# An encoder block on one core: VectorE work reordered at three places of the attention and gate stages

## The chip, the core and the metric

The kernel runs on one core of a Trainium2 chip. A core has five engines, each with its own instruction queue: TensorE (PE; its weight loads are shown apart as PEld), VectorE (DVE), ScalarE (ACT), GpSimd (POOL) and SyncE (SP), which here issues nearly all DMAs. They wait for one another on semaphores. The metric is the device time of one execution in microseconds (us); the median of three runs is given.

## What is computed

One block of a bidirectional encoder for 1024 tokens of 1024 features, in 32-bit floats. Cut to what matters:

```
h    = layer_norm(x)
proj = h @ w_in + b_in                  # split into qa ka va | qb kb vb | ga gb
y_na  = neighbourhood_attention(qa, ka, va, rpb) @ w_branch_na     # 8 heads of 64
y_swa = windowed_gqa_with_sink(qb, kb, vb, sink) @ w_branch_swa    # 8 query heads, 2 key heads
mixed = sigmoid(ga) * y_na + sigmoid(gb) * y_swa
h = layer_norm(ALPHA * h + mixed @ w_out + b_out)
h = layer_norm(ALPHA * h + square(relu(h @ w_ff1 + b_ff1)) @ w_ff2 + b_ff2)
```

## The kernel before

Matmul operands are split into two parts: a high part, the value rounded to the type that PE multiplies fast, and a low part, the rest. A product is three matmuls: high by high, high by low, low by high. So every operand costs ACT a rounding copy (high) and DVE a subtraction (low). Partial sums lie in PSUM, in banks of 128 x 512: four tags (`mm`, `s`, `t`, `o`) of two banks each.

The order of the work on every engine is written out by hand (`manual_schedule`): what the code calls first stands first in its engine's queue.

**Attention.** 16 heads of 4 steps each, 64 steps; the first 8 heads are the windowed ones, the last 8 the neighbourhood's. Step `s` (function `steps`) issues, in this order:

- `part_a2(s + 1)`: DVE turns the sums of exponentials into reciprocals (L592, L593) and scales two tiles of weights with them (L596).
- `part_a(s + 2)`: PE computes scores in two `s` banks (L559, L560); DVE adds the mask or bias, writes the tile out and takes the row maxima (L562), then their negative (L566, L568). These read the banks and so free them.
- a first share of the pumps (below), then a flush of early deferred work,
- `part_b(s)`: PE turns the weights (transposes, L618) into two `t` banks; ACT copies them rounded (`pth`, L621); between, `part_e` lets ACT take the exponentials of step `s + 2` (L580, L583); then DVE takes the low parts (`ptl`, L624), which free the `t` banks; then a flush,
- a second share of the pumps,
- `part_c(s - 1)`: PE multiplies weights and values (L654) into an `o` bank, which takes two steps. After the second, ACT copies one half of the bank's partitions into `oT` (L660), and DVE adds the other half to it (L663, the output addition); then a flush and the last share of the pumps.

A pump is one matmul (L283) of the projections, which fill PE between the attention's own matmuls. A step has 12 pumps in the first 8 heads and 18 in the last 8. Work on a projection's result is deferred: `defer(n, f, ...)` puts `f` on a list to be called at the first flush after `n` more pumps. A flush goes through the list; the flush ahead of `part_b` takes only entries marked early.

For the neighbourhood's q and k (`proj_na_qk`), each half projection ends in `evac` (three copies on ACT) and, four pumps later, `evac2` (three operations on DVE: the low part of q, L358, that of k, L360, and a copy of the latter, L362). The first two read the `mm` bank of the projection and so free it. Both are marked early.

**Gates.** After the attention the remaining columns of the gates' projection are multiplied by a seven-product scheme: operands A11 to A22 and the sums S1 to S4 of activations against sums of weights. `g_sums` forms a weight sum on DVE (L856), `g_hi` rounds it on ACT (L872), `g_lo` takes its low part on DVE (L876), `g_mm` multiplies (L886), and `g_after` brings a result out: a copy on ACT (L946) or an addition on DVE (L926). The sums of activations use helper `f_add` (L926 too). Product 7 uses S3, which is formed into the place of an operand used up, `hT`, in two halves of 1024 columns: ACT rounds both (L1045), then DVE takes both low parts. Products 7 and 4 of one weight block use one bank, with the addition of product 7's result in between.

After the gates come the branch projections, the output projection with its layer norm, and the two feed-forward matrices in the same seven-product scheme. The change touches nothing there.

Of the kernel before, what the change touches and what calls it, by code (L numbers as in the profile page):

```python
# [13 lines left out]
ALU = mybir.AluOpType  # L14
# [33 lines left out]
D_NA = 4  # L48
# [35 lines left out]
def encoder_block(ctx, tc, x, w_in, w_br, w_out, w_ff1, w_ff2, par, rows, rpbp,  # L84
# [4 lines left out]
    def b32(ap):  # L89
        return ap.bitcast(F32)  # L90
# [12 lines left out]
    def psum(tag):  # L103
        return pp.tile([P, 512], F32, tag=tag, name=f"ps_{tag}", bufs=PSB[tag])
# [153 lines left out]
    def h_perm(part, k, half):  # L258
        return hT[:, part, k, half * 512:(half + 1) * 512]
# [17 lines left out]
    def gemm3_steps(ps, w, act):  # L277

        hi, lo = w[:2]
        for k in range(NK):  # L280
            for i, (a, b) in enumerate(((hi, 0), (hi, 1), (lo, 0))):
                yield
                PE.matmul(ps, a[:, k, :], act(b, k), start=(k == 0 and i == 0), stop=(k == NK - 1 and i == 2))  # L283
# [6 lines left out]
    def defer(*fns, pe=False, early=False):  # L290

        later.append([fns[0], fns[1:], pe, early])
# [48 lines left out]
    def proj_na_qk(h, w, store):  # L341
        q = ap.tile([P, S], F32R, tag="q", name="q", bufs=3)
        kh = ap.tile([P, S], F32R, tag="kh", name="kh")
        kl = ap.tile([P, S], F32R, tag="kl", name="kl")
        store.append((q, kh, kl))
        bq, bk = prm[0:64, C_QK + h:C_QK + h + 1], prm[64:P, C_QK + h:C_QK + h + 1]
        for half in range(2):
            cs = slice(half * 512, (half + 1) * 512)
            ps = psum("mm")
            yield from gemm3_steps(ps, w, lambda part, k: h_perm(part, k, half))  # L350

            def evac(cs=cs, ps=ps):
                ACT.activation(q[0:64, cs], ps[0:64, :], AF.Identity, bias=bq, scale=1.0)
                ACT.activation(kh[64:P, cs], ps[64:P, :], AF.Identity, bias=bk, scale=1.0)
                ACT.activation(kh[0:64, cs], ps[64:P, :], AF.Identity, bias=bk, scale=1.0)

            def evac2(cs=cs, ps=ps):
                DVE.scalar_tensor_tensor(out=q[64:P, cs], in0=ps[0:64, :], scalar=bq, in1=b32(q[0:64, cs]),  # L358
                                         op0=ALU.add, op1=ALU.subtract)
                DVE.scalar_tensor_tensor(out=kl[64:P, cs], in0=ps[64:P, :], scalar=bk, in1=b32(kh[64:P, cs]),  # L360
                                         op0=ALU.add, op1=ALU.subtract)
                DVE.tensor_copy(kl[0:64, cs], b32(kl[64:P, cs]))  # L362
            defer(0, evac, D_NA, evac2, early=True)


    mk = ap.tile([P, 640], F32, tag="mk", name="mk", bufs=1)
# [20 lines left out]

    n_rope = [0]
    in_steps, rope_ops = [], []

    def rope_step(p):

        if rope_ops:
            j = cp.tile([P, 1], F32, tag="junk", name="junk", bufs=2)
            POOL.tensor_copy(j, p[:, 0:1])
            rope_ops.pop(0)()
            if len(rope_ops) % 5 == 1:
                rope_ops.pop(0)()
                if rope_ops:
                    defer(8, rope_ops.pop(0))  # L400
# [184 lines left out]
    def part_a2(s):  # L585
        if s >= 64:
            return
        hd, t = heads[s // 4], s % 4
        pns, st = hd.pairs[t]
        sink_h = hd.get()[4]  # L590
        if sink_h is not None:
            DVE.tensor_tensor(out=st[:, 4:6], in0=st[:, 4:6], in1=st[:, 6:8], op=ALU.add)  # L592
        DVE.reciprocal(out=st[:, 6:8], in_=st[:, 4:6])  # L593
        for i in range(2):
            p, n, c0 = pns[i]
            DVE.tensor_scalar(out=p[:, :n], in0=p[:, :n], scalar1=st[:, 6 + i:7 + i], scalar2=None, op0=ALU.mult)  # L596
        rope_step(p)
# [29 lines left out]
    def part_c(s):  # L627

        hd, t = heads[s // 4], s % 4
        order, pth, ptl = hd.pairs[t]  # L630
        _, vv, vi, _, _, o_chunk, o_row = hd.get()
        if t % 2 == 0:
            hd.po = psum("o")
        po = hd.po

        runs = []
        for u, (c, i) in enumerate(order):
            if runs and runs[-1][0] == c:
                runs[-1][2] += 1
            else:  # L640
                runs.append([c, u, 1, i])
        runs.sort(key=lambda r: -r[2])
        runs.append(runs.pop(1))
        cols_ = (t % 2) * 256
        nmm = 0
        for c, u, w, i in runs:
            cc = slice(cols_ + i * P, cols_ + (i + w) * P)
            vs = vv[:, c, vi, :, :].rearrange("p a f -> p (a f)")
            main = (po[:, cc], vs, pth[:, u:u + w, :].rearrange("p u f -> p (u f)"))
            corr = (po[0:64, cc], vs[:, 0:64], ptl[:, u:u + w, :].rearrange("p u f -> p (u f)"))  # L650
            nmm += 1
            lastrun = nmm == len(runs)
            for m in ((corr, main) if lastrun else (main, corr)):
                PE.matmul(*m, start=(nmm == 1 and m is main), stop=(lastrun and m is main))  # L654
        if t % 2 == 1:

            oo = oT[o_row:o_row + 64, o_chunk, (t // 2) * 512:(t // 2 + 1) * 512]

            def evac():
                ACT.copy(oo, po[64:P, :])  # L660

            def evac2():
                DVE.tensor_tensor(out=oo, in0=po[0:64, :], in1=oo, op=ALU.add)  # L663
            if s == 63:
                last_evac.extend((evac, evac2))
            else:
                evac()
                defer(0, evac2)

    def fills():  # L670
        def na_v_of(hp):
# [28 lines left out]
    with tc.manual_schedule(engines=MANUAL):  # L700
# [22 lines left out]
        def pump(n):  # L723
            for _ in range(n):
                if next(fill, "end") == "end":
                    for e in later:
                        e[0] = 0
                    flush()
                    return
                for e in later:  # L730
                    e[0] -= 1
# [52 lines left out]
        def steps(s, n, before_b=None, before_c=None):  # L784

            part = [int(n * SPLIT[0]), int(n * SPLIT[1])]
            part.append(n - sum(part))
            if 0 <= s + 1 < 64:
                part_a2(s + 1)
            if s + 2 < 64:  # L790
                part_a(s + 2)
            pump(part[0])
            if before_b:
                before_b()
            flush(False, True)
            if 0 <= s < 64:
                part_b(s, lambda: part_e(s + 2))
            elif s < 0:
                part_e(s + 2)
            flush(False)  # L800
            pump(part[1])
            if before_c:
                before_c()
            if s >= 1:
                part_c(s - 1)
            flush()
            pump(part[2])
# [45 lines left out]
        def g_sums(p, i):  # L853

            def sub(out, a, b):
                DVE.tensor_tensor(out=out, in0=a, in1=b, op=ALU.subtract)  # L856
            if i == 6:
                gT2[p] = gp.tile([P, 4, P], F32, tag="ts", name="gT2")
                sub(gB(p, 1, 1), gB(p, 1, 2), gB(p, 1, 1))
                sub(gT2[p], gB(p, 2, 2), gB(p, 1, 1))  # L860
            elif i == 7:
                sub(gB(p, 1, 2), gB(p, 2, 2), gB(p, 1, 2))
            elif i == 4:
                sub(gB(p, 2, 1), gB(p, 2, 1), gT2[p])
# [4 lines left out]
        def g_hi(p, i, src=None):  # L869
            gtags.append(gtags.pop(0))  # L870
            t = gw[p, i] = wp.tile([P, 2, 4, P], F32R, tag=gtags[-1], name="gw", bufs=1)
            ACT.copy(t[:, 0], g_src(p, i) if src is None else src)  # L872

        def g_lo(p, i, src=None):
            t = gw[p, i]
            DVE.tensor_tensor(out=t[:, 1], in0=g_src(p, i) if src is None else src, in1=b32(t[:, 0]), op=ALU.subtract)  # L876
# [13 lines left out]
        gop = dict(A11=hT[:, :, K1, T1], A12=hT[:, :, K2, T1], A22=hT[:, :, K2, T2], S3=hT[:, :, K1, T2])  # L890
# [34 lines left out]
        def f_add(out, a, b, op=ALU.add):  # L925
            DVE.tensor_tensor(out=out, in0=a, in1=b, op=op)  # L926
# [10 lines left out]
        g2 = gt[:, 0].rearrange("p (a x) -> p a x", a=4)  # L937
# [103 lines left out]
        g_lo(3, 3)  # L1041
        g_do(2, 5)
        g_do(3, 5)
        for ks in (slice(0, 2), slice(2, 4)):
            ACT.copy(gop["S3"][:, 0, ks], g2[:, ks])  # L1045
        g_sums(2, 7)
        g_sums(3, 7)
        g_hi(2, 7)
        for ks in (slice(0, 2), slice(2, 4)):
            f_add(gop["S3"][:, 1, ks], g2[:, ks], b32(gop["S3"][:, 0, ks]), ALU.subtract)  # L1050
        g_lo(2, 7)
        g_hi(3, 7)
        g_lo(3, 7)
        g_sums(2, 4)
# [1006 lines left out]
```

## Time and profile before

| | |
|---|---|
| median of three runs | 1334.39 us (1333.94 to 1335.63) |
| profiled execution | 1334.06 us |
| its span, first to last instruction | 1332.3 us |
| granted TensorE clock, mean | 0.998 |
| PE busy | 1309.4 us, 6296 matmuls |
| DVE busy | 985.0 us |
| ACT busy | 710.1 us |
| POOL busy | 282.4 us |
| attention, first score product to last | about 91 to 436 us of the span |

The profile is one execution. Times in it are us from the span's start; a row of a timeline gives start, duration, engine, line, operation, what is written and read, the shape, how many instructions were merged, and in brackets the idle time of the engine before it with what ended it. The ends of matmuls are modelled: one of 128 x 512 is shown with some 0.39 us, while the next starts 0.23 after it. So PE's busy share overstates how full it is, and idle time of PE is shown a little too short. A wait that has several causes is put down to the one that came last.

### The profile page before, as it was taken

To read this page: it belongs to the slowest core of one execution; us is meant where nothing else is said; L and a number is where in the kernel's file an instruction comes from. 1 tells how busy PE (TensorE), PEld (TensorE's weight loads), DVE (VectorE), ACT (ScalarE), POOL (GpSimd) and SP (SyncE) were. 2 spreads that over 40 slices of the span, in tenths; PEclk is the share of its full clock that TensorE was granted. 3 is DMA by queue.
4 is the path that set the end of the run, shared out by engine and by line. 5 is a ranking of instruction groups with operands and counts; after the bars stand their busy time and mean duration, and the time that the engine had idled before them with its cause. 6 is when DMAs were issued, how large, how long until landed. Compare 5 with 4: busy or idle time off the path is not lost.

```text
span 1332.3 us, 17348 instructions
## 1 busy us (share of the span) xinstructions
PE 1309.4 (98%) x6296; PEld 1088.7 (82%) x6296; DVE 985.0 (74%) x1618; ACT 710.1 (53%) x1231; POOL 282.4 (21%) x279
## 2 busy tenths in 40 slices
PE   8999998999999999999999999999999999999997
PEld 6788787888888878888888888888888888888886
DVE  7758888877877896444678987677655768787778
ACT  6446666766665535542445755555555543333346
POOL 4441221121120000344540012222100001111207
PEclk9999999999999999999999999999999999999999
DMA  6521111102101323656143576655528644544323
GB/s 226 187 87 49 48 52 41 38 23 47 51 23 40 127 94 118 223 190 221 70 152 134 169 242 205 210 196 187 205 100 311 221 190 150 213 150 174 127 103 127
DMA packets 66422, 183.94 MB, mean 138 GB/s; under 512 B 10400, under 2 KB 12064, under 8 KB 60576
## 3 DMA queue, kind: packets, MB, share of 16 engines
q1 hardware_dynamic: 65904, 182.38, 39.7%
q8 instruction: 49, 0.80, 0.3%
q10 hardware_dynamic: 432, 0.46, 0.1%
q14 instruction: 37, 0.30, 0.1%
HBM read 126.69 MB, written 56.31 MB: 137 GB/s over the span
## 4 chain that ended last, share of the span: by engine, by line
PE 80%; DVE 12%; ACT 3%; issue 1%; POOL 1%; DMA 1%; SPq 0%; DVEq 0%; ACTq 0%; POOLq 0%
PE ps_mm L283 13%; PE ps_mm L1351 7%; PE ps_t L1351 6%; PE ps_o L1351 6%; PE ps_mm L1784 6%; PE ps_s L1784 6%; PE ps_o L1784 5%; PE ps_t L1784 5%; PE ps_s L1351 3%; PE ps_t L618 2%; DVE ss L562 2%; PE ps_o L654 2%; ACT ss L580 2%; PE ps_mm L886 1%; DVE ss L596 1%
## 5 line engine op out<-in xcount | busy, mean ns | idle before, releaser
L283 PE MATMUL ps_mm<-hT,whi 128*128 128x512 f32 x832 | 269.5, 398 | 2.6 <-POOL hT L255 2.1
L283 PEld LDWEIGHTS ps_mm<-hT,whi 128*128 128x128 f32 x832 | 153.6, 188 | 30.2 <-POOL hT L255 3.5
L283 PE MATMUL ps_mm<-hT,wlo 128*128 128x512 f32 x416 | 166.9, 401 | 1.0 <-DVE wlo L717 1.0
L580 ACT ACTIVATE ss<-ss,st 128x384 f32<-128x384 f32 (+1 forms) x128 | 74.5, 583 | 62.1 <-DVE st L568 47.3
L1650 ACT CAST t<-stg 128x2048 fp32r<-128x2048 f32 x28 | 53.5, 1912 | 81.9 <-PE ps_o L1784 46.3
L1803 POOL TENSOR_TENSOR acc<-acc,rst 128x512 f32<-128x512 f32 x16 | 31.0, 1934 | 293.2 <-DMA rst<-xr_d 280.7
L1784 PE MATMUL ps_mm<-t,t 128*128 128x512 f32 x384 | 89.6, 389 | 0.0
L1784 PE MATMUL ps_s<-t,t 128*128 128x512 f32 x384 | 89.6, 389 | 0.0
L283 PEld LDWEIGHTS ps_mm<-hT,wlo 128*128 128x128 f32 x416 | 78.3, 188 | 12.4 <-DVE wlo L717 1.5
L1784 PEld LDWEIGHTS ps_mm<-t,t 128*128 128x128 f32 x384 | 72.1, 188 | 14.9
L1784 PEld LDWEIGHTS ps_s<-t,t 128*128 128x128 f32 x384 | 72.1, 188 | 14.9
L1351 PE MATMUL ps_t<-hS,tw 128*128 128x512 f32 x348 | 83.6, 389 | 0.0
L1351 PEld LDWEIGHTS ps_t<-hS,tw 128*128 128x128 f32 x348 | 65.3, 188 | 13.5
L621 ACT CAST pth<-ps_t 128x384 fp32r<-128x384 f32 (+1 forms) x128 | 51.8, 454 | 43.9 <-PE ps_t L618 43.2
L1653 DVE TENSOR_TENSOR t<-stg,t 128x2048 fp32r<-128x2048 f32 x28 | 65.6, 2341 | 12.9 <-ACT t L1650 12.9
L624 DVE TENSOR_TENSOR ptl<-ps_t,pth 128x384 fp32r<-128x384 f32 (+1 forms) x128 | 61.2, 517 | 17.1 <-ACT pth L621 16.5
L1173 POOL TENSOR_TENSOR mx<-sg 128x512 f32<-128x512 f32 x16 | 33.4, 2089 | 187.8 <-DVE sg L1172 187.8
L1784 PE MATMUL ps_t<-t,t 128*128 128x512 f32 x288 | 67.8, 390 | 0.6 <-DVE t L1653 0.6
L1784 PE MATMUL ps_o<-t,t 128*128 128x512 f32 x288 | 67.2, 389 | 0.0
L1784 PEld LDWEIGHTS ps_t<-t,t 128*128 128x128 f32 x288 | 53.9, 188 | 12.6 <-DVE t L1653 1.5
L1784 PEld LDWEIGHTS ps_o<-t,t 128*128 128x128 f32 x288 | 54.1, 188 | 11.2
L1627 POOL TENSOR_TENSOR rst<-rst,rr 128x512 f32<-128x512 f32 x16 | 22.4, 1400 | 187.3 <-DMA rst<-xn_d 116.0
(307 smaller groups left out, 3159.1 us busy)
## 6 DMA issues: line engine op xcount, KB each, us to landing
us_d<-usl SPq DMA_DIRECT2D x112, 256.0 KB
stg<-us_d SPq DMA_DIRECT2D x28, 1024.0 KB
raw<-in_w_ff SPq DMA_DIRECT2D x36, 512.0 KB
raw<-in_w_in SPq DMA_DIRECT2D x28, 512.0 KB
sg<-sg_d SPq DMA_DIRECT2D x32, 256.0 KB
w2b<-in_w_ff SPq DMA_DIRECT2D x7, 1024.0 KB
w2a<-in_w_ff SPq DMA_DIRECT2D x5, 1024.0 KB
sg_d<-sa SPq DMA_DIRECT2D x16, 256.0 KB
```

The costliest lines, as they stand in the source:

```text
L283: PE.matmul(ps, a[:, k, :], act(b, k), start=(k == 0 and i == 0), stop=(k == NK - 1 and i == 2))
L562: DVE.tensor_tensor_reduce(out=p[:, :n], in0=ps[:, :n], in1=bias_of(j), scale=1.0, scalar=NEG, op0=ALU.add, op1=ALU.max, accum_out=st[:, i ...
L580: ACT.activation(p[:, :n], p[:, :n], AF.Exp, bias=st[:, 2 + i:3 + i], scale=0.125, accum_out=st[:, 4 + i:5 + i])
L618: PE.transpose(pt[:, (u - a) * P:(u - a + 1) * P], p[:, (c - c0) * P:(c - c0 + 1) * P], ident)
L621: ACT.copy(pth[:, a:b, :], pv)
L624: DVE.tensor_tensor(out=ptl[:, a:b, :], in0=pv, in1=b32(pth[:, a:b, :]), op=ALU.subtract)
L1173: POOL.tensor_tensor(out=mx[:, f, half * 512:(half + 1) * 512], in0=both[0], in1=both[1], op=ALU.add)
L1351: PE.matmul(ps, ww, act[:, part, k, :], start=(first and k == 0 and m == 0), stop=(k == 3 and m == 2), skip_group_check=True)
L1650: ACT.copy(slot[:, :, 0, :], src)
L1653: DVE.tensor_tensor(out=slot[:, :, 1, :], in0=src, in1=b32(slot[:, :, 0, :]), op=ALU.subtract)
L1784: PE.matmul(ps, st[:, a, part, j * P:(j + 1) * P], w[:, a, wpart, :], start=(first and a == 0 and m == 0), stop=(a == 3 and m == 2), skip_ ...
L1803: POOL.tensor_tensor(out=z, in0=z, in1=t, op=ALU.add)
```

## The change

Three edits; nothing is computed differently, and the instructions of every engine are the same in number.

1. *Low parts of the neighbourhood's q and k.* `evac2` was marked early always; now it is early only if the step at which `evac` is called is 32 or later. Before step 32 it waits for the flush behind `part_b`.
2. *Output additions.* The addition was deferred by 0 pumps and so called in the flush right behind `part_c`; now it is deferred by 14.
3. *Last gate operand.* Instead of rounding both halves of S3 and later taking both low parts, each half is rounded and its low part taken at once, and the low part of product 7's weights (first block) stands between the halves.

```diff
-            defer(0, evac, D_NA, evac2, early=True)
+            defer(0, lambda: (evac(), defer(D_NA, evac2, early=step_now[0] >= 32)), early=True)
...
+    step_now = [0]
...
                 evac()
-                defer(0, evac2)
+                defer(14, evac2)
...
             part.append(n - sum(part))
+            step_now[0] = s
...
-        for ks in (slice(0, 2), slice(2, 4)):
+        def s3_part(ks):
             ACT.copy(gop["S3"][:, 0, ks], g2[:, ks])
+            f_add(gop["S3"][:, 1, ks], g2[:, ks], b32(gop["S3"][:, 0, ks]), ALU.subtract)
         g_sums(2, 7)
         g_sums(3, 7)
+        s3_part(slice(0, 2))
         g_hi(2, 7)
-        for ks in (slice(0, 2), slice(2, 4)):
-            f_add(gop["S3"][:, 1, ks], g2[:, ks], b32(gop["S3"][:, 0, ks]), ALU.subtract)
         g_lo(2, 7)
+        s3_part(slice(2, 4))
         g_hi(3, 7)
         g_lo(3, 7)
```

The order of the instructions on PE, POOL and SP is the same as before; on ACT one pair changes places (the second half of S3 and the rounding of product 7's weights); the rest is on DVE. Line numbers from L390 on are larger by one to three in the changed kernel.

DVE in the fourth head, where an output addition stood behind `part_b`'s low parts (`ps_o_1492` is the bank that it reads), before:

```order
L624 TENSOR_TENSOR ptl_1526<-ps_t_1527,pth_1525 128x384
L624 TENSOR_TENSOR ptl_1526<-ps_t_1531,pth_1525 128x384
L663 TENSOR_TENSOR oT_844<-ps_o_1492,oT_844 64x512
L592 TENSOR_TENSOR st_1510<-st_1510 128x2
L593 RECIPROCAL st_1510<-st_1510 128x2
```

And the same place now:

```order
L625 TENSOR_TENSOR ptl_1525<-ps_t_1526,pth_1524 128x384
L625 TENSOR_TENSOR ptl_1525<-ps_t_1530,pth_1524 128x384
L664 TENSOR_TENSOR oT_844<-ps_o_1368,oT_844 64x512
L593 TENSOR_TENSOR st_1509<-st_1509 128x2
L594 RECIPROCAL st_1509<-st_1509 128x2
```

An addition still stands there, but it reads the bank before, `ps_o_1368`, whose addition was called two steps earlier until now. With 12 pumps a step, 14 pumps put each addition to the flush behind `part_b` of the next step but one. With 18 pumps it moves by ten rows, behind the next step's maxima and low parts.

DVE at the first low parts of the neighbourhood's q and k that moved, before:

```order
L568 TENSOR_SCALAR st_2415<-st_2415,snk8_106 128x2
L358 SCALAR_TENSOR_TENSOR q_2262<-ps_mm_2265,prm_104,q_2262 64x512
L360 SCALAR_TENSOR_TENSOR kl_2264<-ps_mm_2265,prm_104,kh_2263 64x512
L362 CAST kl_2264<-kl_2264 64x512
L624 TENSOR_TENSOR ptl_2434<-ps_t_2435,pth_2433 128x384
L624 TENSOR_TENSOR ptl_2434<-ps_t_2439,pth_2433 128x384
L592 TENSOR_TENSOR st_2415<-st_2415 128x2
```

And now:

```order
L569 TENSOR_SCALAR st_2414<-st_2414,snk8_106 128x2
L625 TENSOR_TENSOR ptl_2430<-ps_t_2431,pth_2429 128x384
L625 TENSOR_TENSOR ptl_2430<-ps_t_2435,pth_2429 128x384
L358 SCALAR_TENSOR_TENSOR q_2262<-ps_mm_2265,prm_104,q_2262 64x512
L360 SCALAR_TENSOR_TENSOR kl_2264<-ps_mm_2265,prm_104,kh_2263 64x512
L362 CAST kl_2264<-kl_2264 64x512
L593 TENSOR_TENSOR st_2414<-st_2414 128x2
```

The two low parts of the turned weights stand ahead of q and k instead of behind. This happens three times; all later groups stand where they stood.

DVE in the gate stage, from the weight sums of product 7 on (`gw_5328` and `gw_5333` are the weights of product 7 of the two blocks, `hT` is S3), before:

```order
L856 TENSOR_TENSOR graw_5114<-graw_5114 128x512
L856 TENSOR_TENSOR gt_5113<-gt_5113 128x512
L926 TENSOR_TENSOR hT_84<-gt_5113,hT_84 128x2x512 x2
L876 TENSOR_TENSOR gw_5328<-graw_5114,gw_5328 128x512
L876 TENSOR_TENSOR gw_5333<-gt_5113,gw_5333 128x512
```

And now:

```order
L858 TENSOR_TENSOR graw_5114<-graw_5114 128x512
L858 TENSOR_TENSOR gt_5113<-gt_5113 128x512
L928 TENSOR_TENSOR hT_84<-gt_5113,hT_84 128x2x512
L878 TENSOR_TENSOR gw_5328<-graw_5114,gw_5328 128x512
L928 TENSOR_TENSOR hT_84<-gt_5113,hT_84 128x2x512
L878 TENSOR_TENSOR gw_5333<-gt_5113,gw_5333 128x512
```

The low part of the first block's weights has moved ahead of the second half of S3; what follows is as before.

## The prediction

> **What bounds the kernel now.** I read the page's first part first, then the waits of TensorE (PE) and VectorE (DVE), then the busy time by stretch, and last the timelines at the places that the change touches. The page gives PE as all but full:
>
> ```profile
> PE 1309.4 (98%) x6296; PEld 1088.7 (82%) x6296; DVE 985.0 (74%) x1618; ACT 710.1 (53%) x1231; POOL 282.4 (21%) x279
> ```
>
> A share over the whole span hides where PE stands still. The view of busy time by stretch, cut so that each stretch is one attention head (four steps, from a score product to the one four steps later), then one step, another step, and 80 us of the later heads, shows it. Columns: the stretch, its length, then busy us and instructions of PE, PE's weight loads, DVE, ACT, POOL.
>
> ```profile
> 106.72:125.63 18.91, 18.91 (x115) 16.33 (x114) 16.50 (x49) 13.15 (x35) 2.12 (x3) 1.00 0.19 68
> 125.63:144.84 19.21, 19.04 (x115) 16.39 (x114) 16.84 (x52) 13.38 (x35) 4.75 (x8) 1.00 0.00 1
> 144.84:165.97 21.13, 19.99 (x115) 16.17 (x115) 18.54 (x52) 13.27 (x35) 3.79 (x5) 1.00 0.22 76
> 165.97:185.29 19.32, 19.19 (x115) 16.53 (x115) 16.95 (x52) 13.38 (x35) 4.77 (x8) 1.00 0.00 1
> 185.29:206.82 21.53, 19.98 (x115) 16.11 (x115) 18.94 (x52) 13.27 (x35) 8.00 (x12) 1.00 0.36 108
> 206.82:228.52 21.70, 20.70 (x122) 17.55 (x123) 16.65 (x53) 14.88 (x38) 1.79 (x3) 1.00 0.15 35
> 228.52:249.09 20.57, 19.52 (x115) 16.36 (x114) 18.54 (x54) 15.53 (x38) 0.58 (x2) 1.00 0.09 26
> 249.09:256.39 7.30, 6.49 (x37) 5.24 (x36) 7.07 (x18) 6.32 (x16) 2.57 (x6) 1.00 0.11 20
> 256.39:262.56 6.17, 6.17 (x36) 5.36 (x35) 5.89 (x17) 3.16 (x8) 1.17 (x1) 1.00 0.04 8
> 360.00:440.00 80.00, 79.99 (x458) 69.16 (x457) 59.63 (x159) 47.74 (x112) 8.29 (x15) 1.00 0.14 43
> ```
>
> The first head is clean: 115 matmuls in 18.91 us, PE never idle. Heads with the same 115 take 0.30, 2.22, 0.41, 2.62 and 1.66 us more. The head at 206.82 has 122; seven more at the mean of the first row (18.91/115 = 0.16) are 1.15, so 1.64 of its 2.79 are waiting. The step at 249.09 takes 1.13 more than its neighbour. Together **10.0 us**, all between 125 and 256 us; from there PE is full (79.99 of 80). That is all that the attention can give.
>
> The waits between 120 and 260 us say whom PE waits for, and what DVE itself waits for (us in total, times, longest):
>
> ```profile
> PE ps_s L559 <- DVE st L562: 2.9, 3, 1.5
> PE ps_t L618 <- DVE ptl L624: 1.8, 2, 1.0
> DVE oT L663 <- ACT oT L660: 6.2, 7, 1.1
> ```
>
> PE waits for DVE: for the maxima (L562), which empty the score banks, and for the low parts of the turned weights (L624), which empty the transposes' banks. And DVE, the late one, stands 6.2 us before the output addition (L663), with work queued behind it.
>
> **Output additions (14 pumps later).** DVE at one addition and around the next but one, and ACT beside that:
>
> ```profile
> 132.22 0.68 DVE L663 TENSOR_TENSOR oT<-ps_o,oT 64x512 f32<-64x512 f32 x1 [1.14 <-ACT oT L660]
> ...
> 151.24 0.54 DVE L624 TENSOR_TENSOR ptl<-ps_t,pth 128x384 fp32r<-128x384 f32 x1
> 152.92 0.68 DVE L663 TENSOR_TENSOR oT<-ps_o,oT 64x512 f32<-64x512 f32 x1 [1.14 <-ACT oT L660]
> 153.53 0.14 DVE L592 TENSOR_TENSOR st<-st 128x2 f32<-128x2 f32 x1
> 157.72 0.16 DVE L592 TENSOR_TENSOR st<-st 128x2 f32<-128x2 f32 x1 [0.77 <-ACT st L583]
> ```
>
> ```profile
> 152.00 0.28 ACT L583 ACTIVATE st<-st,prm 128x2 f32<-128x2 f32 x1
> 156.19 0.62 ACT L580 ACTIVATE ss<-ss,st 128x384 f32<-128x384 f32 x1 [1.95 <-DVE st L568]
> ```
>
> DVE is done at 151.24 + 0.54 = 151.78 and waits 1.14 for ACT's half of the output. The sums behind it (L592) had their input at 152.00 + 0.28 = 152.28. After the change the addition that stands here is the one of the pair of steps before, whose operands were ready long ago. It takes its 0.61 (152.92 to 153.53) at once, and L592 starts about 1.14 us sooner. No work is saved: each place still holds one addition, only an older one; what goes is the wait. The next idle time, 0.77 at 157.72, is the round trip maxima, exponentials, sums; ACT itself stood idle 1.95 us before it, waiting for DVE, so it follows and the 1.14 carries on.
>
> Where it ends, DVE's and PE's rows:
>
> ```profile
> 161.06 1.22 DVE L515 TENSOR_TENSOR wlo<-raw,whi 128x1024 fp32r<-128x1024 f32 x1
> ...
> 163.70 0.68 DVE L663 TENSOR_TENSOR oT<-ps_o,oT 64x512 f32<-64x512 f32 x1
> ```
>
> ```profile
> 163.17 0.28 PE L654 MATMUL ps_o<-pth,vv 128*128 128x256 f32 x1
> ...
> 163.99 0.39 PE L283 MATMUL ps_mm<-hT,wlo 128*128 128x512 f32 x1
> 164.22 0.61 PE L283 MATMUL ps_mm<-hT,whi 128*128 128x512 f32 x2
> 165.97 0.39 PE L559 MATMUL ps_s<-kh,q 128*128 128x256 f32 x1 [1.13 <-DVE st L562]
> ```
>
> Matmuls of this size start 0.23 apart (163.99 to 164.22), so PE could have gone on at 164.68 and stood 1.29. The addition at 163.70 leaves, but another goes in behind `ptl`, ahead of the weights' low part at 161.06 and so ahead of the same maxima: 0.61 for 0.61. So these maxima come sooner by DVE's vanished waits alone. Of the seven, five are of 1.14 and two of 0.25 (5.7 + 0.5 = 6.2): two of the five lie before the stall at 165.97 (132.22 and 152.92, above), two between it and the end of the head at 206.82, one after. DVE has no slack between them, since the small stalls of PE there are waits for DVE too. Before 165.97: 2 x 1.14 = 2.28 of the 0.30 + 2.22 = 2.52 that the two heads lost. Before 206.82: 2.28 of 0.41 + 2.62 = 3.03. **Term: 4.56 us**; bounds 2.28 (the first idle time of each pair is lost in slack) and 5.55 (all of the four heads' loss).
>
> Later heads: 18 pumps a step, PE full, so additions that move there cost or save nothing. What hides them is DVE's share, 59.63 of 80 in the last row above. Without that cover 19 additions at 0.61 would cost up to 11.6; I take 0.
>
> The bank that an addition empties is now free later, and the first product of the second next pair waits for that. At 163.17 PE takes a bank whose addition now stands ahead of the row at 161.06 and ends at 161.06 + 0.61 = 161.67. That leaves 1.5 us; I take 0.
>
> **Low parts of the neighbourhood's q and k.** In spite of its title this part makes nothing earlier: they were early at every step, and from step 32 on still are. Before step 32 they now stand behind `ptl` instead of ahead. This moves three groups of three DVE instructions. At the first, rows of DVE, ACT and PE:
>
> ```profile
> 228.41 0.74 DVE L358 SCALAR_TENSOR_TENSOR q<-ps_mm,prm,q 64x512 fp32r<-64x512 f32 x1
> 229.17 0.76 DVE L360 SCALAR_TENSOR_TENSOR kl<-ps_mm,prm,kh 64x512 fp32r<-64x512 f32 x1
> ...
> 230.41 1.02 DVE L624 TENSOR_TENSOR ptl<-ps_t,pth 128x384 fp32r<-128x384 f32 x2
> ```
>
> ```profile
> 226.69 0.86 ACT L621 CAST pth<-ps_t 128x384 fp32r<-128x384 f32 x2
> ```
>
> ```profile
> 229.36 0.63 PE L283 MATMUL ps_mm<-hT,whi 128*128 128x512 f32 x2
> 231.02 0.79 PE L618 MATMUL ps_t<-ident,ss 128*128 128x128 f32 x4 [1.03 <-DVE ptl L624]
> 251.57 1.01 PE L618 MATMUL ps_t<-ident,ss 128*128 128x128 f32 x6 [0.81 <-DVE ptl L624]
> ```
>
> `ptl` had its input at 226.69 + 0.86 = 227.55 and starts at 230.41 behind 2.00 us of q and k. Put first, it starts at 228.41, and PE's transposes go at 229.36 + 2 x 0.23 = 229.82 instead of 231.02: **1.20**. The work before the next maxima is the same. The second group costs PE less (1.66 - 1.20 leaves 0.46; I take 0.3), the third 0.81 + 0.16 = 0.97 (idle time as shown counts from a modelled end that overlaps 0.16: 164.22 + 0.61 - 0.16 is 164.67, near the 164.68 above). What is late next is the bank of the projection, which q and k empty: PE's next half, right behind the transposes, now waits for them. At the first group they have read it at 228.41 + 0.94 + 0.74 + 0.76 = 230.85, and PE comes at 229.82 + 1.01 = 230.83, so nothing is lost. At the third PE comes earlier by what it has gained till then, so I count 0.5 of 0.97, an estimate. With 0.4 from the head at 206.82 (its DVE idles too) **the term is 2.4**; bounds 1.2 and 4.4 (1.64 + 1.66 + 1.13).
>
> **Last gate operand in halves.** Rows of DVE, then PE (the halves are L926 into hT; gw is the weights' low parts, go the additions to the results):
>
> ```profile
> 489.08 2.35 DVE L926 TENSOR_TENSOR hT<-gt,hT 128x1024 fp32r<-128x1024 f32 x2
> 491.35 0.68 DVE L876 TENSOR_TENSOR gw<-graw,gw 128x512 fp32r<-128x512 f32 x1
> ...
> 496.64 1.46 DVE L926 TENSOR_TENSOR go<-ps_o,go 128x512 f32<-128x512 f32 x2
> ```
>
> ```profile
> 490.42 0.61 PE L886 MATMUL ps_o<-hT,gw 128*128 128x512 f32 x2
> 492.09 6.08 PE L886 MATMUL ps_o<-hT,gw 128*128 128x512 f32 x24 [1.06 <-DVE gw L876]
> 496.98 1.42 PE L886 MATMUL ps_o<-hT,gw 128*128 128x512 f32 x4
> ```
>
> Two matmuls, then PE waits for the low part at 491.35. With one half of 1.13 behind it instead of ahead it is done at about 490.9, and PE gains 1.1 to 1.2 there. But the product after the next accumulates into the bank that the addition at 496.64 reads: four matmuls from 496.98 take 1.42 where 3 x 0.23 + 0.39 = 1.08 would do, a wait of 0.34 that ends with that addition (496.64 + 0.68). DVE's work up to it is the same in sum, only in another order, so it ends when it did. PE comes 1.1 sooner and waits 1.1 longer. **Term: 0**; bounds 0 and 1.2.
>
> **Sum.** 4.56 + 2.4 + 0 = 7.0 us off the profiled execution's 1334.06 (span 1332.3), so 1327.1. The runs' median, 1334.39, is 0.33 above that execution; from it, **1327.4 us**. PE, POOL and SP keep their order, so no transfer moves against another.
>
> **Rivals.** *Half of it* (1330.6): DVE catches up by itself before each big stall, so one idle time of each pair counts, 2.28, and of the second term 1.5. For it: the 0.77 round trips, where a gain could drown. Against: ACT's 1.95 of idle in the same place. Chance 0.18.
>
> *No change* (1334.4): DVE is simply full, 18.54 of 21.13 and 18.94 of 21.53, and every vanished wait comes back as a wait for ACT's exponentials. Against: 18.54 us of work fit into the clean 18.91. Chance 0.13, with the case that the gains are given back later. The page's 98% speaks for it. [...]
>
> *The gate pays too* (1326.2): the wait at 497 is not for that addition. Against: its end fits. Chance 0.08.
>
> *Slower* (1338): the output banks. Each of some ten products at the start of a pair now waits for an addition that DVE does two steps later. It decides if DVE runs more than about 1.5 us later against PE than now (163.17 against 161.67); then each costs up to 0.61, 6 us in all, less what the second term gives (1.2 to 2.4). Against: DVE gains on PE. Chance 0.04.
>
> **How the numbers follow.** Forecast, 5.5 to 9.0 saved: 0.57. Range: from 9.5 saved (both upper bounds, 5.55 + 4.4, less the 0.47 that the third group can't give) past the half case (3.8) to 2.7, the least that can be told from no change: 1324.9 to 1331.7. No change and slower lie outside, 0.17 in all. What a measurement of this kernel can tell from no change is about 0.2%, 2.7 us. Faster by more than that: 0.57 + 0.08 + most of the half = 0.81; the same 0.14; slower 0.05.
>
> **What would show it.** Right: in the profile after, the DVE waits for ACT at the output addition are gone; the four heads to 206.82 take about 4.5 us less; the transposes at 231 and 251 don't wait for `ptl`; the wait at 492 is gone and one of about 1.3 stands five microseconds later. Wrong: heads of 21 us as before with DVE idle ahead of L592, or products into ps_o (L654) that wait for the output addition.

## The result, and the profile after

| | before | after |
|---|---|---|
| median of six runs | 1335.6 us (1333.94 to 1335.9) | 1326.95 us (1326.68 to 1328.14) |
| profiled execution, its span | 1334.06, 1332.3 us | 1328.14, 1326.4 us |
| four heads, steps 8 to 23 | 81.19 us | 75.72 us |
| steps 24 to 32 | 49.57 us | 46.78 us |
| steps 33 to 59 | 167.21 us | 167.20 us |

The ratio is 0.994 (0.9927 to 0.9953): 8.65 us less by the medians. The spans differ by 5.9 us only, because the profiled execution of after is the slowest of its six and its first score product comes 2.06 us later (93.33 against 91.27 us), before anything that the change touches; in the twelve runs below that start lies anywhere between 90.7 and 93.4 us. At 11.70 us PE ends a wait of 1.93 us for ACT (1.08 us in before, ending at 10.83), and then its granted clock is one half for 3.4 us, from 13 us on, where it stays at 1.00 in before; the last section comes back to this. So the stretches are compared by their lengths, not by the spans.

First the busy time by stretch of after, cut at the same score products as in the prediction (stretch, length, then busy us and instructions of PE, PE's weight loads, DVE, ACT, POOL, then the clock, the DMA's share and GB/s):

```profile
127.70:146.53 18.83, 18.83 (x116) 16.55 (x114) 17.57 (x53) 13.87 (x38) 5.69 (x8) 1.00 0.09 23
146.53:165.36 18.83, 18.83 (x115) 16.55 (x114) 17.30 (x50) 12.73 (x33) 2.86 (x4) 1.00 0.19 63
165.36:184.20 18.84, 18.84 (x116) 16.55 (x115) 17.59 (x53) 13.78 (x36) 5.72 (x8) 1.00 0.07 19
184.20:203.42 19.22, 19.00 (x115) 16.36 (x113) 17.72 (x49) 13.14 (x35) 4.69 (x7) 1.00 0.34 103
203.42:224.51 21.09, 20.33 (x123) 17.55 (x124) 17.50 (x55) 15.96 (x41) 3.50 (x7) 1.00 0.13 36
224.51:243.33 18.82, 18.82 (x116) 16.54 (x115) 17.39 (x51) 13.58 (x34) 0.08 (x1) 1.00 0.04 11
243.33:250.20 6.87, 6.42 (x38) 5.35 (x36) 6.50 (x18) 6.07 (x17) 2.89 (x7) 1.00 0.20 65
```

The heads of 21.13 and 21.53 us are now 18.83 and 19.22, and the heads beside them are full as well (18.83 and 18.84). What is left of the 10.0 us: 0.4 at the end of the fourth head, about 1.0 in the head at 203.42, 0.7 at 243.33.

The waits between 120 and 260 us, first PE's, then DVE's:

```profile
PE ps_t L328 <- DVE ptl L625: 0.6, 1, 0.6
PE ps_mm L283 <- DVE kl L360: 0.5, 1, 0.5
PE ps_s L560 <- DVE st L563: 0.2, 1, 0.2
```

```profile
DVE st L593 <- ACT st L584: 4.4, 6, 0.8
DVE vv L332 <- ACT vv L331: 1.7, 1, 1.7
DVE ptl L625 <- ACT pth L622: 0.7, 1, 0.7
```

The 6.2 us at the output addition are gone. No row has a product waiting for an addition (`ps_o` for `oT`). At the place shown in the prediction, DVE now:

```profile
151.71 0.68 DVE L664 TENSOR_TENSOR oT<-ps_o,oT 64x512 f32<-64x512 f32 x1
152.42 0.16 DVE L593 TENSOR_TENSOR st<-st 128x2 f32<-128x2 f32 x1
```

The addition starts at 151.71, right behind `ptl`, and the sums 0.71 later; before, the same rows had 1.14 of waiting in them.

The gate stage of after, PE and then DVE:

```profile
484.24 5.85 PE L888 MATMUL ps_o<-hT,gw 128*128 128x512 f32 x24
491.27 5.69 PE L888 MATMUL ps_o<-hT,gw 128*128 128x512 f32 x24 [1.18 <-DVE go L928]
...
524.52 0.39 PE L273 MATMUL ps_t<-oS,whi 128*128 128x512 f32 x1
```

```profile
490.44 1.28 DVE L928 TENSOR_TENSOR go<-ps_o,go 128x512 f32<-128x512 f32 x2
```

Product 7 runs through without a wait, and then, 5.9 us later, product 4 waits 1.18 for the addition at 490.44. From the last score product (436.05) to the first product of the branch projection (524.52) it is 88.47 us.

### The profile page after: what moved, and what is told of

It reads as the page before. It is cut to its first block, busy times and chain, and to the rows that moved or that the text cites. A ratio compares the mean times of both kernels' runs of the same rounds, so it can differ in the third digit from the quotient of the medians.

```text
span 1326.4 us, 17358 instructions
## 1 busy us (share of the span) xinstructions
PE 1307.1 (99%) x6296; PEld 1090.9 (82%) x6296; DVE 988.7 (75%) x1618; ACT 710.3 (54%) x1231; POOL 281.7 (21%) x279
## 4 chain that ended last, share of the span: by engine, by line
PE 82%; DVE 12%; ACT 3%; issue 1%; POOL 1%; DMA 1%; SPq 0%; DVEq 0%; ACTq 0%; POOLq 0%
PE ps_mm L283 14%; PE ps_mm L1354 7%; PE ps_o L1354 6%; PE ps_t L1354 6%; PE ps_mm L1787 6%; PE ps_s L1787 6%; PE ps_o L1787 5%; PE ps_t L1787 5%; PE ps_s L1354 3%; PE ps_o L655 2%; PE ps_t L619 2%; PE ps_mm L888 1%; DVE ss L563 1%; PE ps_s L1245 1%; PE ps_s L1244 1%
## 5 line engine op out<-in xcount | busy, mean ns | idle before, releaser
L1656 DVE TENSOR_TENSOR t<-stg,t 128x2048 fp32r<-128x2048 f32 x28 | 68.3, 2440 | 12.6 <-ACT t L1653 12.6
```

The source lines that it names most:

```text
L1656: DVE.tensor_tensor(out=slot[:, :, 1, :], in0=src, in1=b32(slot[:, :, 0, :]), op=ALU.subtract)
```

## Experiments

The theory to be tested: the time came from DVE's wait for ACT at the output additions, and from `ptl` ahead of q and k; the gate edit and the later heads give nothing. Rivals: that it is the additions' place in DVE's order that pays, that the low parts pay by themselves, that the gate edit pays.

All runs in one table. Ratios are to runs of the kernel before on the same chip (medians 1334.46 to 1334.97 us; for after, the 1335.6 above); the last two columns are sums of the view by stretch, the four heads of steps 8 to 23 and steps 24 to 32.

| kernel | median, us | ratio (interval) | 8 to 23 | 24 to 32 |
|---|---|---|---|---|
| before | | | 81.19 | 49.57 |
| after | 1326.95 | 0.994 (0.9927 to 0.9953) | 75.72 | 46.78 |
| additions alone | 1326.82 | 0.9939 (0.9927 to 0.9952) | 75.95 | 47.10 |
| low parts alone | 1333.54 | 0.9991 (0.9982 to 0.9999) | 81.19 | 48.67 |
| gate edit alone | 1334.35 | 1.0 (0.9991 to 1.0009) | 81.16 | 49.57 |
| additions, wait kept | 1342.55 | 1.0061 (1.0048 to 1.0075) | 87.28 | 50.92 |
| additions by 4 pumps | 1326.69 | 0.9934 (0.9921 to 0.9948) | 75.33 | 47.55 |
| additions from step 32 | 1334.15 | 0.9997 (0.9988 to 1.0006) | 81.20 | 49.55 |
| operand of the pair before | 1334.49 | 0.9998 (0.999 to 1.0007) | 81.17 | 49.50 |
| after, q and k never early | 1327.07 | 0.9942 (0.9928 to 0.9955) | 76.02 | 46.95 |
| after, one gate move | 1326.67 | 0.9937 (0.9924 to 0.9951) | 76.05 | 46.95 |
| after, two gate moves | 1325.27 | 0.9927 (0.9914 to 0.9939) | 76.06 | 47.03 |
| same, 4 pumps | 1325.89 | 0.9932 (0.992 to 0.9945) | 75.33 | 48.46 |
| same, 4 then 14 pumps | 1325.22 | 0.9929 (0.9916 to 0.9943) | 75.50 | 46.98 |

### The three edits one by one

```diff
-                defer(0, evac2)
+                defer(14, evac2)
```

> The kernel before with the second edit alone (output additions 14 pumps later). My theory: the time goes with VectorE's waits for ScalarE at the additions, five of 1.14 us, nearly all of it between 125 and 206 us of the span. It expects 5.0 to 6.0 us saved of the time before, in the profile the four heads from step 8 to step 23 shorter by 5.4 together, and steps 24 to 32 as before within 0.7. The rival, that VectorE is full there and the gain of the changed kernel needs the low parts of q and k as well (or comes from them), expects under 3 us here.

It saves 7.9 us by the medians, as much as the whole change, and more than expected: the four heads give 5.24, and steps 24 to 32 another 2.47 where I expected at most 0.7. The four heads and the next head of this kernel:

```profile
125.83:201.78 75.95, 75.34 (x458) 65.83 (x456) 70.40 (x202) 53.48 (x140) 20.07 (x29) 1.00 0.16 52
201.78:222.98 21.20, 20.51 (x123) 17.56 (x123) 17.59 (x54) 15.84 (x40) 2.79 (x5) 1.00 0.12 36
```

What the additions do in 24 to 28 is seen in DVE's rows, of this kernel and then of before, around the low part of `vv` (L332), which waits for ACT:

```profile
206.88 0.67 DVE L663 TENSOR_TENSOR oT<-ps_o,oT 64x512 f32<-64x512 f32 x1
209.27 0.69 DVE L332 TENSOR_TENSOR vv<-ps_t,vv 128x512 fp32r<-128x512 f32 x1 [1.72 <-ACT vv L331]
...
217.21 0.68 DVE L663 TENSOR_TENSOR oT<-ps_o,oT 64x512 f32<-64x512 f32 x1
...
219.17 0.69 DVE L332 TENSOR_TENSOR vv<-ps_t,vv 128x512 fp32r<-128x512 f32 x1
```

```profile
214.31 0.69 DVE L332 TENSOR_TENSOR vv<-ps_t,vv 128x512 fp32r<-128x512 f32 x1 [2.31 <-ACT vv L331]
215.03 0.68 DVE L663 TENSOR_TENSOR oT<-ps_o,oT 64x512 f32<-64x512 f32 x1
...
224.73 0.69 DVE L332 TENSOR_TENSOR vv<-ps_t,vv 128x512 fp32r<-128x512 f32 x1 [0.86 <-ACT vv L331]
225.45 0.68 DVE L663 TENSOR_TENSOR oT<-ps_o,oT 64x512 f32<-64x512 f32 x1
```

Before, these two additions stood behind a late `vv` and held up the next maxima by their own 0.6 to 0.7. Now they stand ahead of it, where DVE waits for ACT anyway: 2.31 of idle time became 1.72, 0.86 became none. The steps behind them are 0.52 and 0.82 shorter, 1.34 of the 2.47 together. The other 1.15 lie at steps 30 and 32 (0.37 and 0.78 shorter). Just ahead of them the next two additions waited for ACT in before, and in this kernel neither does; I put the 1.15 to these waits, though no run has them apart. Rows of before:

```profile
235.56 0.68 DVE L663 TENSOR_TENSOR oT<-ps_o,oT 64x512 f32<-64x512 f32 x1 [1.14 <-ACT oT L660]
...
245.81 0.68 DVE L663 TENSOR_TENSOR oT<-ps_o,oT 64x512 f32<-64x512 f32 x1 [0.25 <-ACT oT L660]
```

```diff
-            defer(0, evac, D_NA, evac2, early=True)
+            defer(0, lambda: (evac(), defer(D_NA, evac2, early=step_now[0] >= 32)), early=True)
...
+    step_now = [0]
...
+            step_now[0] = s
```

> The kernel before with the first edit alone (low parts of the neighbourhood's q and k behind those of the turned weights before step 32). My theory: it acts on its own from step 26 on, 1.4 us at step 28 (228 to 234 us), 0.4 at steps 30 and 32 each; in sum 1.8 to 2.8 us saved, steps 8 to 23 as before. The rival, that it pays only when the additions are out of the way, expects under 1 us.

1.2 us by the medians, 0.90 in steps 24 to 32, none before. That is less than my 1.8, and by the steps as small as the rival had it. The stretch of steps 28 to 31 (20.57 us in before), and PE's waits between 120 and 260 us:

```profile
230.49:250.29 19.80, 19.49 (x116) 16.33 (x114) 17.74 (x51) 14.29 (x36) 0.00 (x0) 1.00 0.07 20
```

```profile
PE ps_s L560 <- DVE st L563: 2.7, 2, 1.6
PE ps_mm L283 <- DVE kl L360: 0.8, 2, 0.5
```

The first group gives 1.12 (6.19 to 5.07 at step 28), as worked out, but at two others PE now waits for the projection's bank. The edits overlap: 2.47 and 0.90 apart, 2.79 together. On top of the additions the low parts are worth 0.1 to 0.3 (46.78 to 47.03 in the four kernels with both, the additions at 14 pumps, against 47.10), which the medians (1326.95 against 1326.82) don't show. So the rival's condition, that they pay once the additions are out of the way, fails too. Step by step, they still give 0.59 at step 28 (5.37 with the additions alone, 4.78 in after), and take 0.35 back at step 32 (6.52 and 6.87; 7.00 and 7.01 in the other three), where PE's next half waits for the projection's bank.

```diff
-        for ks in (slice(0, 2), slice(2, 4)):
-            f_add(gop["S3"][:, 1, ks], g2[:, ks], b32(gop["S3"][:, 0, ks]), ALU.subtract)
...
+        s3_part(slice(0, 2))
         g_hi(2, 7)
         g_lo(2, 7)
+        s3_part(slice(2, 4))
```

> The kernel before with the third edit alone (S3 in halves, the weights' low part between). My theory: the wait of TensorE for the low part at 492 us goes, and a wait for the addition to the bank of product 7 takes its place one product later; 0 us saved (within 0.3). The rival, that it pays what the vanished wait shows, expects 1.1 us.

No change, as the theory has it. PE in the gate stage of this kernel:

```profile
492.50 5.87 PE L886 MATMUL ps_o<-hT,gw 128*128 128x512 f32 x24
499.55 0.70 PE L886 MATMUL ps_o<-hT,gw 128*128 128x512 f32 x2 [1.18 <-DVE go L926]
```

The 1.06 at product 7 is gone, and 1.18 stands at product 4.

### The wait, or the place

Here the additions stand where the first experiment put them, in the same order on DVE, but ACT's copy is moved along, so that each addition again waits for a copy that has just been queued behind ACT's exponentials.

```diff
-                evac()
-                defer(0, evac2)
+                defer(14, lambda: (evac(), evac2()))
```

> The kernel before with the additions at their new place (14 pumps later) and ScalarE's copy of the other half moved there with them, so that VectorE's order is that of the run with the additions alone, and each addition waits for a copy queued behind the exponentials again. My theory, that the gain is the vanished wait: in steps 8 to 23 nearly all of the 5.2 us is lost again (under 1 us saved) with waits of about 1.1 us at the additions in the profile; in all under 2.5 us saved. The rival, that the place in VectorE's order pays: as with the additions alone, 7 to 8 us saved.

15.7 us slower by the medians than with the additions alone, with the same order of instructions on DVE, PE and POOL; only ACT's copies stand elsewhere. Its DVE waits between 120 and 260 us, and the row at the known place:

```profile
DVE oT L663 <- ACT oT L660: 16.7, 13, 1.6
```

```profile
154.25 0.69 DVE L663 TENSOR_TENSOR oT<-ps_o,oT 64x512 f32<-64x512 f32 x1 [1.12 <-ACT oT L660]
```

So the place alone gives nothing; the ready operand does. It is even 7.6 us slower than before, which neither theory said: before, 7 of 14 additions waited, 6.2 us in all, and of the others four stood behind 1.2 us of a weights' low part; here 13 wait, up to 1.6. A part of the loss goes with TensorE's lower clock, by an estimate at most 3.4 us (last section).

The other half of the question: the operand ready, at another place.

```diff
-                defer(0, evac2)
+                defer(4, evac2)
```

> The kernel before with the output additions deferred by 4 pumps instead of 14: with 12 pumps a step each comes behind the low parts of the turned weights of the next step, where no addition stood. My theory: its operand is ready there too, so the waits of 1.14 go all the same and steps 8 to 23 save 4.5 to 5.5 us; in steps 24 to 28 up to 1.3 less than with 14, since the additions don't fall into the waits for ScalarE's copy of vv. The rival, that an addition in the other step takes from VectorE what the wait gave, expects under 3 us in steps 8 to 23.

7.9 us saved, as with 14 pumps. The four heads:

```profile
126.55:201.88 75.33, 75.33 (x457) 66.19 (x456) 70.40 (x204) 53.46 (x140) 19.19 (x27) 1.00 0.17 53
```

PE is busy in all of the 75.33. The expected loss of up to 1.3 in steps 24 to 28 did not come (steps 26 and 28 are 0.54 and 0.80 shorter than before): with 4 pumps as with 14, the addition no longer stands behind the late `vv`.

```diff
             def evac2():
-                DVE.tensor_tensor(out=oo, in0=po[0:64, :], in1=oo, op=ALU.add)
+                DVE.tensor_tensor(out=o2, in0=po[0:64, :], in1=o2, op=ALU.add)
+            o2 = oo if s == 63 or not oo_last else oo_last[0]
+            oo_last[:] = [oo]
```

> The kernel before, each output addition at its old place, but adding into the part of oT that the pair before wrote, so that it doesn't need ScalarE's copy of its own pair (the sums in oT come out otherwise than the reference's; the work is the same in number and size). My theory, that the time goes with the wait for ScalarE and not with the place: steps 8 to 23 save about 5.2 us as with the additions moved alone (2.73 + 2.47), and of the 2.45 that those save in steps 24 to 32 about 1.1 come, since the two waits for ScalarE's copy of vv (2.31 and 0.86 us), into which the moved additions fell, stay; 5.5 to 7 us saved in all. The rival, that the place behind the next maxima is what pays, expects under 1.5 us.

0.1 us, and no test of what it was meant for: the wait did not go. DVE in this kernel, between 100 and 262 us:

```profile
DVE oT L664 <- ACT oT L661: 7.3, 8, 1.1
```

The addition no longer reads what ACT's copy writes, but the program still orders the one behind the other. Both read one bank and both write the tile oT; which of the two makes the order was not tested. The run only shows that other data without another order change nothing.

```diff
-                defer(0, evac2)
+                defer(14 if s >= 32 else 0, evac2)
```

> The kernel before, with output additions 14 pumps later only from step 32 on. My theory: TensorE is full there, so 0 us saved or lost (within 0.3) and every step from 33 on as long as before. The rival, that the gain lies in the 18-pump heads too, expects over 1 us.

0 (1334.15 against 1334.57 us), and the steps from 33 on are as long as before.

```diff
-early=step_now[0] >= 32
+early=False
```

> The changed kernel with the low parts of the neighbourhood's q and k behind those of the turned weights at every step, from step 32 on too. My theory: there the transposes don't wait, so nothing is to be had, and the projection's next half can come to wait for its bank, as it did at step 31 of the changed kernel (0.70 us between two starts); 0 to 2 us more than the changed kernel. The rival, that the early place costs there as well, expects over 0.5 us less.

1327.07 us, no different from after; from 255 us on (step 33) PE waits neither at the transposes nor for the projection's bank. The step-32 condition matters for nothing that the runs can tell, and the rival falls with it.

### Following the gate's wait

```diff
-        g_sums(3, 4)
-        g_hi(3, 4)
         g_do(3, 3)
+        g_do(2, 7)
+        g_after(2, 7)
+        g_sums(3, 4)
+        g_hi(3, 4)
         g_after(3, 3)
         g_lo(3, 4)
-        g_do(2, 7)
-        g_after(2, 7)
```

> The changed kernel, and in the gate stage the addition of product 7's result (first block) ahead of the second block's sum, addition and low part, instead of behind them; PE's order as it is. My theory: the addition ends at about 489.1 instead of 491.1 us, PE goes from product 7 to product 4 without the wait of 1.18 us, and what follows comes as much earlier: 1.2 to 1.5 us less than the changed kernel, so 9.8 to 10.2 less than the kernel before. The rival, that the next late operand (product 6's low part at 495.4 us, or ScalarE's copies) takes this gain as well, expects 0 less than the changed kernel.

The rival was right. PE in this kernel:

```profile
482.13 11.27 PE L888 MATMUL ps_o<-hT,gw 128*128 128x512 f32 x48
493.42 3.29 PE L888 MATMUL ps_mm<-gS,gw 128*128 128x512 f32 x12
497.61 2.58 PE L888 MATMUL ps_mm<-gS,gw 128*128 128x512 f32 x9 [0.91 <-ACT gw L874]
```

Products 7 and 4 follow one another, and the wait stands at product 6, ahead of the second of the next two weight blocks. The stage takes 88.5 us again. That wait is for weights whose sum stands on DVE behind a low part of the attention's output, which nobody needs yet. So both moves:

```diff
         g_lo(1, 6)
-        o_lo(1)
         g_hi(1, 5)
         g_sums(0, 6)
         g_hi(0, 6)
         g_lo(0, 6)
+        o_lo(1)
```

> The changed kernel with two moves in the gate stage: the addition of product 7's result ahead of the second block's sum, addition and low part (as in the run before), and the low part of the second chunk of the attention's output behind the preparation of product 6's second weight block instead of ahead. That run showed the wait of TensorE move once more, from 1.18 us at the addition to 0.91 us at product 6's rounded weights. My theory: each of these is a queue on VectorE, and with both out of the way the stage from the last score product to the end of the gates (88.5 us in every kernel so far) takes 0.8 to 1.2 us less. The rival, that the stage ends by something else that holds it at 88.5, expects 88.5 again and a further wait.

PE in this kernel, without a wait:

```profile
483.17 11.29 PE L888 MATMUL ps_o<-hT,gw 128*128 128x512 f32 x48
494.44 6.03 PE L888 MATMUL ps_mm<-gS,gw 128*128 128x512 f32 x24
...
522.06 0.39 PE L273 MATMUL ps_t<-oS,whi 128*128 128x512 f32 x1
```

From the last score product (434.99) to 522.06 it is 87.07 us, 1.40 less than in after. The median, 1325.27 us, is 1.4 to 1.8 below the kernels that save in the attention and have 88.5; the intervals of the ratios overlap, so the gain is shown by the trace and not by the times.

Two tries at combining this with the additions 4 pumps later, first at every step, then up to step 21 only:

```diff
-                defer(14, evac2)
+                defer(4, evac2)
```

> All that paid so far in one kernel: the changed kernel with output additions 4 pumps later instead of 14, and both moves in the gate stage. My theory: the attention saves what the run with 4 pumps saved up to step 27 (2.65 + 3.17 + 0.92) and what the changed kernel saved from step 28 on (1.74 + 0.43), 8.9 us, and the gate stage 1.4; 10.0 to 10.5 us less than the kernel before. The rival, that the places in the other steps cost as much at the q and k groups as they give at step 23, expects 9.3 us, as the run with the two gate moves and 14 pumps.

9.1 us saved, worse than with 14 pumps in the trace by 0.7 (123.79 against 123.09 in the two stretches): PE's waits and the late stretch show why, and the rival was right.

```profile
PE ps_mm L283 <- DVE kl L360: 2.0, 2, 1.4
```

```profile
241.24:249.07 7.83, 6.43 (x38) 5.36 (x37) 7.03 (x18) 6.43 (x17) 2.67 (x7) 1.00 0.16 51
```

An addition now stands right ahead of q and k there (242.71 and 243.40 on DVE), and the projection's bank is freed late.

```diff
-                defer(14, evac2)
+                defer(4 if s < 22 else 14, evac2)
```

> The changed kernel with both moves in the gate stage, and the output additions 4 pumps later up to step 21 and 14 pumps later behind it. My theory: with 4 pumps it was only the places among the q and k groups, from step 28 on, that cost (5.46 us at step 30 and 7.83 at step 32, where 14 pumps gave 4.61 and 7.01), and only step 23 that gained (4.60 where 14 pumps gave 4.99 to 5.50). So steps 8 to 23 save 5.8 us, 24 to 27 0.5 to 0.9, 28 to 32 2.0, the gate stage 1.4: 9.5 to 10.2 us less than the kernel before, 0.3 to 0.9 less than with 14 pumps throughout. The rival, that the gain of step 23 is taken back at the next late place, expects 9.1 to 9.3, as with 14 pumps throughout.

1325.22 us: in the trace 0.6 less in the two stretches together than with 14 pumps, in the medians nothing. This kernel and the one with both gate moves and 14 pumps throughout are the best of the study: 9.2 and 9.3 us below the kernel before, and 1.4 us shorter than after in the gate stage.

## Why the prediction came out right, and where it didn't

The predicted 1327.4 us stands against 1326.95, a sum of 7.0 against 8.65 by the medians and 8.3 in the attention's steps. That the times agree to 0.45 is in part luck: the sum was taken off 1334.39, the median of three runs, and the six runs of before have 1335.6; the saving itself was 1.65 too small.

- *What bounds it*: right. All of the gain lies between 125 and 256 us, and steps 33 to 59 take 167.20 where they took 167.21.
- *Output additions, 4.56*: right mechanism, too small. The four heads gave 5.47 in after and 5.24 with the additions alone, close to the upper bound of 5.55. I counted two idle times of 1.14 for each pair of heads. That these vanish is shown; where the other 0.7 to 0.9 comes from is not, since the additions that did not wait for 1.14 waited 0.05 in all in these heads. PE's whole loss was the better estimate.
- *Low parts, 2.4*: the size came out (2.79 in steps 24 to 32), by luck, and the cause did not; this is the step that failed. Of the 2.79, the additions alone give 2.47, the low parts alone 0.90. Taken by itself the first group is worth the 1.20 that I gave it (1.12), but the second lost 0.35 at steps 30 and 31 where I counted a gain of 0.3, the third gave 0.14 instead of 0.5, and the head at 206.82 gave nothing instead of 0.4. I credited the stall at 231 to the place of q and k alone, by the row that PE waited for. With the additions alone it shrinks as well (step 28 takes 5.37 instead of 6.19): DVE was late there because two additions stood behind a late `vv`. The waits of 2.31 and 0.86 at L332 were in the trace, and I did not ask what stood behind them. And my sum for the additions ended at 206.82, though two of their seven waits, 1.14 and 0.25, lie behind it; I put these at nothing without a reason.
- *The third group's bank*: right that PE's next half waits there. With the additions moved, the low parts cost at that step: it takes 6.87 in after, 6.52 with the additions alone. The row of after:

```profile
246.11 0.73 PE L283 MATMUL ps_mm<-hT,whi 128*128 128x512 f32 x2 [0.45 <-DVE kl L360]
```

- *Gate, 0*: right, with the wait where I put it. That the next one stands right behind it, and that the stage is 88.5 us either way, the prediction did not see.
- *Later heads, 0, and the output banks, 0*: right, by the run with the late heads alone, and by PE's waits in after, in which no product waits for an addition. (In the kernel with the wait kept two do, 0.4 us in all.)
- *Rivals*: "half of it" fell because the idle times carry on, as ACT's 1.95 of idle time said. "No change" fell with the result: the vanished waits did not come back as waits for exponentials, which are 4.4 us between 120 and 260 us in both kernels. "The gate pays too" fell with the gate edit alone, and "slower" with the output banks.

## What to carry to other kernels

When an engine waits in its queue for another engine's queue, as VectorE did for 6.2 us at the additions, first look for an older operand to put there: here the same order of VectorE's instructions with and without a ready operand differed by 15.7 us. Price such an edit by what the waiting engine downstream has lost, not by the single idle times, and ask for each late instruction what stands behind it, since here an addition behind a late instruction held up what follows by its own 0.6 to 0.7 us. Two edits aimed at one lateness need not add up (0.90 and 2.47 apart, at most 2.79 together), and a stall removed from a chain of banks and operands may be gained only when the next ones in the chain have been followed too, as in this gate stage.

## What the runs showed of the hardware

Behind three long waits of PE its granted clock was one half in these traces. In the kernel with the wait kept, PE stood twice for over 2 us; its row at the first, and then the granted clock behind the first in slices of a microsecond (the figure before the DMA's share):

```profile
169.09 0.49 PE L559 MATMUL ps_s<-kh,q 128*128 128x256 f32 x1 [2.40 <-DVE st L562]
```

```profile
169.00:170.00 1.00, 0.91 (x4) 0.91 (x5) 0.96 (x6) 0.32 (x1) 0.00 (x0) 0.61 0.03 8
170.00:171.00 1.00, 1.00 (x4) 0.90 (x3) 1.00 (x4) 1.00 (x5) 0.00 (x0) 0.50 0.00 0
171.00:172.00 1.00, 1.00 (x5) 0.70 (x5) 0.93 (x5) 0.07 (x1) 0.00 (x0) 0.50 0.00 0
172.00:173.00 1.00, 1.00 (x7) 0.96 (x6) 1.00 (x5) 0.54 (x2) 0.75 (x2) 0.69 0.00 0
173.00:174.00 1.00, 1.00 (x6) 0.82 (x5) 0.96 (x2) 0.66 (x2) 0.68 (x1) 1.00 0.00 0
```

The clock goes to one half right behind this wait and is back at 1.00 some 3.5 us later (0.61 and 0.69 are slices in which it changes), and that step takes 6.48 us where it takes 4.99 in before and 4.83 in after. The same follows the wait of 2.96 at 213 (0.50 from 214 to 217 us). Before, with waits of up to 1.55 us, the clock stays at 1.00 in every stretch shown. So part of this kernel's 15.7 us is the clock: two stretches of 3.4 us at half speed can cost PE up to 1.7 us each, an estimate from their lengths.

The third is the wait of 1.93 us for ACT in after that ends at 11.70 us. The clock is at 0.50 from 13 to 16 us there, and the transposes start 0.21 us apart (13.86 to 14.07), where they start 0.11 apart until then (11.86 to 11.97). In before the wait at this place is 1.08 us, and the clock stays at 1.00. Over their whole spans the kernels with the low parts alone, with the gate edit alone and with q and k never early have a mean clock of 0.997, 0.997 and 0.996, after and the kernel with the wait kept 0.996, all others 0.998. Together with after, the first three come latest to their first score product (93.1 to 93.4 us). Neither the length of a wait nor anything else was varied by itself to see what sets the clock.

Step 23 took 4.99 us in after and 5.50 in the kernel with one gate move, though their attention is the same code. The scaling of the two tiles of weights took 1.06 in the one and 1.19 in the other there, against 0.75 at 157 in after; why, no run settles. The difference sets the size of what can be read from one trace of this kernel: about half a microsecond.
